# Sample-state updates as four 32-row matmuls on four row groups, with keys and values laid out through DRAM

## The chip, the core and the metric

The kernel runs on one core of a Trainium2 chip. A core has five engines that work at the same time and wait for each other by semaphores: PE (TensorE, matmuls; PEld is its weight load), DVE (VectorE), ACT (ScalarE), POOL (GpSimd) and SP (SyncE, which here only issues DMA transfers). SBUF is the on-chip memory of 128 partitions; PSUM holds matmul results in eight banks of 128 partitions by 512 fp32 numbers. TensorE is an array of 128 rows (over which a matmul sums) by 128 columns; a matmul may use a part of the rows (a row group of 32 or 64) or of the columns (a column group). The metric is device time in microseconds, the median of three runs.

## The reference

One layer of a hybrid decoder is computed for a prompt (512 tokens) and for a sample batch (8 sequences of 4 new tokens): an input projection, an mLSTM branch with 4 heads of dimension 512, a sliding-window attention branch, a gated merge and a layer norm. The change touches the sample's mLSTM only. For each of 8 sequences and 4 heads there is a matrix memory C of 512 by 512 that is read and updated:

```python
num = einsum('bhts,bhsd->bhtd', s, v) + inter[..., None] * einsum('bhtk,bhkv->bhtv', q, C)
...
C_new = decay[..., None, None] * C + einsum('bhsk,bhsv->bhkv', w[..., None] * k, v)
```

So every C tile (1 MB) is loaded, multiplied with 4 queries, updated by a product of 4 weighted keys with 4 values, and stored. The output C is returned for all 32 pairs of sequence and head. All numbers are fp32; to keep that precision in TensorE's faster fp32r format, operands are split into a high and a low part and the needed products of parts are summed.

## The kernel before

The large projections take most of the time. `paired` (L695) goes through a list of pairs of output column blocks; for each pair it runs seven half products (`half_product`, L654: sixteen matmuls at L662 and eight at L664, 272 columns each) that use three PSUM banks, with sums of weight blocks (`prepare`, L642), splits of weights (`split`, L198 on ACT and L199 on DVE) and a gathering of the results (`gather`, L672 to L691) around them. Splits are prepared up to three half products ahead (L704).

After each half product, `tick()` (L127) lets each generator in `live` run up to its next `yield`. That is how smaller work is mixed into the projections. `samples()` (L1208) is one such generator: it takes the heads one after another and runs `sample_head` (L1155). A planner that simulates the engines then sets the final order of each engine's instructions from dependences and priorities; `tc.high_priority` moves instructions ahead in it, and `tc.issue_after` puts an instruction behind a named one on its engine. Each engine, and each DMA queue, then works strictly in that order. All transfers of this part are issued by SP.

`sample_prep` (L1060) loads queries, keys and values of a head (L1065), and makes two tiles of 128 rows by 512: `kA` (L1092 and L1093) holds the weighted keys of all 32 tokens four times, as high, high, low and low parts; `V4` (L1102 and L1105) holds the values as high, low, high and low parts. A product over the 128 rows is so a sum over 32 tokens and over all four pairs of parts.

`sample_head` then loops over the 8 sequences b. A C tile is loaded one sequence ahead (L1057). POOL makes `qz` (L1172, L1173), the queries of b among zeros, and `Ab` (L1175), which is `kA` with the rows of all other sequences set to zero by a mask. Four matmuls (L1188) on the four column groups of the array multiply the queries with the four 128-row parts of C and add into the PSUM bank `pC`, which is held for the whole head; they come up in the profile as eight records. Then, for each of the four parts of C, one matmul of 128 rows, 128 columns and 512 moving columns (L1194) makes the update, though only 16 of its 128 rows are not zero, and one DVE instruction (L1195) scales the C tile by the decay and adds it. Two parts are done in one tick and two in the next. The stores (L1165) are issued by SP in the next sequence's turn. `sample_finish` (L1133) works on `pC` at the end of a head.

PSUM banks come from two pools of four: `sm()` (L104), which the sample's work uses, `pC` and the update's results among it, and `bank()` (L214), which the half products use.

Of the kernel before, what the change touches and what calls it, by code (L numbers as in the profile page):

```python
# [15 lines left out]
F32 = mybir.dt.float32  # L16
F32R = mybir.dt.float32r
# [22 lines left out]
SLOPES = [float(np.float32(2.0 ** (-8.0 * (h + 1) / AH))) for h in range(AH)]  # L40


C_ID, C_TRI, C_M8, C_SM, C_SEL, C_DIST, C_SB, C_Q, C_N = 0, 128, 256, 264, 296, 328, 584, 716, 844


def constants():
    c = np.zeros((128, C_N), np.float32)
    p = np.arange(128)
    c[:, C_ID:C_ID + 128] = np.eye(128)
    c[:, C_TRI:C_TRI + 128] = np.where(p[None, :] >= p[:, None], 0.0, NEG)  # L50
    dist = p[:, None] + 128 - np.arange(256)[None, :]
    c[:, C_DIST:C_DIST + 256] = np.where((dist >= 0) & (dist < 128), dist, 1.0e32)
    t = p % 4
    sd = 128 + t[:, None] - np.arange(132)[None, :]
    slope = np.array(SLOPES, np.float32)[p // 4]
    sb = -(slope[:, None] * sd.astype(np.float32)).astype(np.float32)
    c[:, C_SB:C_SB + 132] = np.where((sd >= 0) & (sd < 128), sb, NEG)
    tok = p % 32
    c[:, C_M8:C_M8 + 8] = (tok[:, None] // 4 == np.arange(8)[None, :])
    tt = np.arange(32)  # L60
    same = (tok[:, None] // 4 == tt[None, :] // 4) & (tok[:, None] <= tt[None, :])
    c[:, C_SM:C_SM + 32] = np.where(same, 0.0, NEG)
    c[:, C_SEL:C_SEL + 32] = (tok[:, None] == tt[None, :])
    c[:, C_Q:C_Q + 128] = np.where(tok[:, None] == tok[None, :], 0.25, 0.0)
    return c

# [7 lines left out]
def _build(tc, nc, i, o, es):  # L74
# [25 lines left out]
    def nm(s):  # L100
        count[0] += 1
        return f"{s}_{count[0]}"

    def sm():  # L104
        return psB.tile([128, 512], F32, tag="sm", name=nm("sm"))
# [4 lines left out]
    def r32(ap):  # L110
        return ap.bitcast(F32)
# [62 lines left out]
    d_t = dr.tile([16, 128, T], F32, name="d_t")  # L174
    d_y = dr.tile([16, 128, T], F32, name="d_y")
    d_o = dr.tile([12, 128, T], F32, name="d_o")

    def kview(name):
        return i[name].rearrange("(kt p) c -> p kt c", p=128)
# [860 lines left out]
    sp = {}  # L1040

    def open_samples():
        for name, bufs in (("s1p", 1), ("sC", 2), ("sw", 2)):
            sp[name] = pool(esS, name, bufs)

    def st1(shape, tag, dt=F32, p="s1p"):
        return sp[p].tile(shape, dt, tag=tag, name=nm(tag))
# [2 lines left out]
        return r32(st1([128, 512], "rep", F32R)[:])  # L1050

    def w512():
        return sp["sw"].tile([128, 512], F32, tag="w", name=nm("w"))

    def load_C(h, b):
        ct = sp["sC"].tile([128, 4, 512], F32, tag="C", name=nm("C"))
# [3 lines left out]
    def sample_prep(h, r):  # L1060
        qs = st1([128, 4, NS], "qs", p="sw")
        ks_, vs = (st1([128, 4, NS], t_) for t_ in ("ks", "vs"))
        hc = slice(h * 4, h * 4 + 4)
        for t_, d_ in ((qs, d_q), (ks_, d_k), (vs, d_v)):
            nc.sync.dma_start(t_[:], d_[hc, :, SEQ:T].rearrange("c p t -> p c t"))  # L1065
        nh_ = w512()
        nh = nh_[:8]
        nc.sync.dma_start(nh, i["state_mlstm_n"][:, h, :])
        yield
        yield  # L1070
        rep = rep_tile()
        G.tensor_copy(rep.rearrange("p (c r t) -> p c r t", c=4, r=4), ks_[:].unsqueeze(2).to_broadcast([128, 4, 4, NS]))
        yield

        pS, pb = sm(), sm()
        for c in range(4):
            PE.matmul(pS[:, 0:NS], rep[:, c * 128:c * 128 + 128], qs[:, c], start=(c == 0), stop=(c == 3))
        PE.matmul(pb[:, 0:NS], row_h[:, h:h + 1].to_broadcast([68, 128]), nM[:, SEQ:T], start=True, stop=True)
        pk = sm()
        for c in range(4):  # L1080
            PE.transpose(pk[:, c * 128:c * 128 + 128], rep[:, c * 128:c * 128 + 128], ident)
        ds = st1([128, NS], "ds")
        V.tensor_tensor(out=ds[:], in0=pb[:, 0:NS], in1=cc[:, C_SM:C_SM + NS], op=ALU.add)
        A.activation(ds[:], ds[:], AF.Exp, bias=colT1[:, 4, 0, h:h + 1])
        V.tensor_tensor(out=ds[:], in0=pS[:, 0:NS], in1=ds[:], op=ALU.mult)
        Pst = st1([128, NS], "Pst", F32R)
        A.copy(Pst[:], ds[:])
        V.tensor_tensor(out=Pst[64:128], in0=ds[64:128], in1=r32(Pst[64:128]), op=ALU.subtract)

        wcol = colT2[:, 4, 2, h:h + 1]  # L1090
        kA = st1([128, 512], "kA", F32R)
        A.activation(kA[:], pk[:], AF.Copy, scale=wcol)  # L1092
        V.scalar_tensor_tensor(kA[64:128], pk[64:128], wcol[64:128], r32(kA[64:128]), op0=ALU.mult, op1=ALU.subtract)  # L1093
        repv = rep_tile()
        G.tensor_copy(repv.rearrange("p (c r t) -> p c r t", c=4, r=4), vs[:].unsqueeze(2).to_broadcast([128, 4, 4, NS]))
        yield

        pvv = sm()
        for c in range(4):
            PE.transpose(pvv[:, c * 128:c * 128 + 128], repv[:, c * 128:c * 128 + 128], ident)  # L1100
        V4 = st1([128, 512], "V4", F32R)
        A.copy(V4[:], pvv[:])  # L1102
        for q in (1, 3):
            rr = slice(q * 32, q * 32 + 32)
            V.tensor_tensor(out=V4[rr], in0=pvv[rr], in1=r32(V4[rr]), op=ALU.subtract)  # L1105

        pn = sm()
        for c in range(4):
            PE.transpose(pn[:, c * 8:c * 8 + 8], nh[:, c * 128:c * 128 + 128], ident[:8, :8])
        nT = st1([128, 4, NB], "nT")  # L1110
        V.tensor_copy(nT[:].rearrange("p c b -> p (c b)"), pn[:, 0:32])
        yield
        pq = sm()
        for c in range(4):
            PE.matmul(pq[:NS, 0:NB], qs[:, c], nT[:, c], start=(c == 0), stop=(c == 3))
        pd = sm()
        PE.matmul(pd[:NS, 0:2], Pst[:], ones_r[:], start=True, stop=True)
        pnn = sm()
        PE.matmul(pnn[:8, :], m8r[:], kA[:], start=True, stop=True)
        den = st1([32, 16], "den", p="sw")  # L1120
        V.scalar_tensor_tensor(den[:, 0:8], pq[:NS, 0:NB], colT2[0:32, 4, 1, h:h + 1], cc[0:32, C_M8:C_M8 + 8],
                               op0=ALU.mult, op1=ALU.mult, accum_out=den[:, 8:9])
        V.tensor_tensor(out=den[:, 9:10], in0=pd[:NS, 0:1], in1=den[:, 8:9], op=ALU.add)
        V.scalar_tensor_tensor(nh, nh, dcc[:, h:h + 1], pnn[:8, :], op0=ALU.mult, op1=ALU.add)
        nc.sync.dma_start(n_s[:, h, :], nh)
        yield
        pN = sm()
        PE.matmul(pN[:NS, :], Pst[:], V4[:], start=True, stop=True)
        num = st1([32, 512], "num")[:]
        A.copy(num, pN[:NS, :])  # L1130
        r.update(kA=kA, V4=V4, den=den, num=num, qs=qs)

    def sample_finish(h, r, pC):  # L1133
        qh, ql = (st1([128, 512], t_, F32R) for t_ in ("rep", "qcl"))
        col = colT2[:, 4, 1, h:h + 1]
        A.activation(qh[:], pC[:], AF.Copy, scale=col)
        V.scalar_tensor_tensor(ql[:], pC[:], col, r32(qh[:]), op0=ALU.mult, op1=ALU.subtract)
        gs = st1([128, 4, NS], "gs", p="sw")
        nc.sync.dma_start(gs[:], d_g[h * 4:h * 4 + 4, :, SEQ:T].rearrange("c p t -> p c t"))
        yield  # L1140
        num, den = r["num"], r["den"]
# [13 lines left out]
    def sample_head(h):  # L1155
# [12 lines left out]
        for b in range(NB):  # L1168
            ct = nxt

            qz = st1([128, 4, NS], "qz", p="sw")
            G.memset(qz[:], 0.0)  # L1172
            G.tensor_copy(qz[:, :, b * 4:b * 4 + 4], r["qs"][:, :, b * 4:b * 4 + 4])  # L1173
            Ab = st1([128, 512], "rep", F32R)
            G.tensor_scalar(Ab[:], r32(r["kA"][:]), cc[:, C_M8 + b:C_M8 + b + 1], None, op0=ALU.mult)  # L1175
            for j in range(4 + b % 2):
                yield
                if j == 0:
                    store()
                elif j == 2 and b + 1 < NB:  # L1180
                    with tc.issue_after(state["load"].ins):
                        nxt = load_C(h, b + 1)
            if b == 0:
                pC = sm()

            with tc.high_priority(offset=3000):
                for c in range(4):
                    PE.matmul(pC[c * 32:c * 32 + 32, :], qz[:, c], ct[:, c],  # L1188
                              start=(b == 0), stop=(b == NB - 1), tile_position=(0, c * 32))
            for c in range(4):  # L1190
                if c == 2:
                    yield
                pu = sm()
                PE.matmul(pu[:], Ab[:, c * 128:c * 128 + 128], r["V4"][:], start=True, stop=True)  # L1194
                V.scalar_tensor_tensor(ct[:, c], ct[:, c], dcb[:, h, b:b + 1], pu[:], op0=ALU.mult, op1=ALU.add)  # L1195
                if c % 2:
                    stores.append((C_s[b, h, (c - 1) * 128:c * 128 + 128, :].rearrange("(c p) v -> p c v", p=128),
                                   ct[:, c - 1:c + 1]))
        yield
        store()  # L1200
        while h not in gated:
# [669 lines left out]
```

## Time and profile before

| what | value |
|---|---|
| median of three runs | 2505.25 us (2504.25 to 2505.31) |
| span of the profiled execution, first to last instruction | 2501.3 us |
| mean granted TensorE clock | 0.997 |
| PE busy, weight loads busy | 2467.7 us, 2410.1 us |
| DVE, ACT, POOL busy | 1817.9, 1242.3, 388.8 us |
| memory traffic | 457.36 MB, mean 183 GB/s |
| first to last update matmul (L1194) | 1077.2 to 1757.4 us |
| update matmuls, C scale-and-add on DVE | 128 each |

The profile is of one execution; its span does not hold what lies before the first and after the last instruction, so it is 3.95 us below the median; no other time of that execution is given. Busy times of different engines overlap. Rows name the line, engine, operation and tiles (`out<-in`); a tile stands under the name it was made with, so the update's PSUM tile is `sm`, its keys (`Ab`) are `rep` and its values (`V4`) are `V`. A shape such as `128*32` before the element counts of a matmul is the rows and columns of the array that it uses. `A <- B` in a list of waits says that A waited for B.

### The profile page before, as it was taken

The numbers are of one execution on the slowest core, as the hardware profiler recorded it, in microseconds if no ns is written. First come the engines' busy times: TensorE is split into PE (matmuls) and PEld (weight loads), VectorE is DVE, ScalarE is ACT, GpSimd is POOL, SyncE is SP. The second block draws the span as 40 slices with busy tenths as digits, with TensorE's granted clock in tenths as the row PEclk, the third lists the DMA queues.
The fourth block names the chain that finished last, engine by engine and source line by source line (L and its number), as shares of the span: only waits on it lengthen the run. The fifth ranks groups of instructions, "written<-read, shape, count | busy, mean of one in ns | idle before, by whom it ended". The sixth has DMA issues, their size and how long they took to land.

```text
span 2501.3 us, 48664 instructions
## 1 busy us (share of the span) xinstructions
PE 2467.7 (99%) x19542; PEld 2410.1 (96%) x19542; DVE 1817.9 (73%) x2785; ACT 1242.3 (50%) x2033; POOL 388.8 (16%) x376
## 2 busy tenths in 40 slices
PE   8999999999999999999999999999999999999997
PEld 8899999999999999999999999999999999999997
DVE  7867677677677687787877888787855654766667
ACT  6457677666667665443433444444633333334431
POOL 2111221121121111121111122211000000110101
PEclk9999999999999999999999999999999999999998
DMA  6677666666666655477677567577745546788776
GB/s 166 153 185 187 149 152 159 156 146 164 153 148 161 149 126 150 113 208 226 184 216 222 168 198 216 172 221 216 247 157 177 193 146 213 210 228 257 211 217 195
DMA packets 551796, 457.36 MB, mean 183 GB/s; under 512 B 45073, under 2 KB 451777, under 8 KB 551313
## 3 DMA queue, kind: packets, MB, share of 16 engines
q1 hardware_dynamic: 534672, 394.73, 53.2%
q0 software_dynamic: 15696, 57.15, 11.8%
q8 instruction: 153, 2.51, 0.4%
q10 hardware_dynamic: 1200, 2.36, 0.3%
q14 instruction: 75, 0.61, 0.1%
HBM read 313.82 MB, written 94.22 MB: 163 GB/s over the span
## 4 chain that ended last, share of the span: by engine, by line
PE 49%; issue 4%; DMA 2%; DVE 2%; ACT 0%; SPq 0%; POOL 0%; DVEq 0%; POOLq 0%; ACTq 0%
PE bank L662 22%; PE bank L664 11%; PE bank L207 6%; PE sm L1375 2%; PE sm L1194 1%; PE sm L1188 1%; PE sm L1407 1%; PE sm L1420 1%; PE sm L207 1%; PE sm L1737 1%; DMA tx<-d_y 1%; DMA ty<-d_y 0%; DMA d_y<-c 0%; DMA tx<-d_brm 0%; DVE wl L199 0%
## 5 line engine op out<-in xcount | busy, mean ns | idle before, releaser
L198 ACT CAST wh<-raw 128x1024 fp32r<-128x1024 f32 x632 | 661.6, 1048 | 820.6 <-PE bank L662 680.1
L199 DVE TENSOR_TENSOR wl<-raw,wh 128x1024 fp32r<-128x1024 f32 x632 | 779.7, 1234 | 238.5 <-ACT wh L198 205.6
L662 PE MATMUL bank<-xk,wh 128*128 128x272 f32 x2336 | 322.6, 288 | 1.4 <-DVE ev L687 1.4
L642 DVE TENSOR_TENSOR raw<-raw,raw 128x1024 f32<-128x1024 f32 x238 | 302.9, 1275 | 8.2 <-DMA raw<-in_w_in 2.2
L662 PEld LDWEIGHTS bank<-xk,wh 128*128 128x128 f32 x2336 | 304.0, 188 | 3.5 <-DVE ev L687 1.6
L681 POOL TENSOR_TENSOR ev<-p,ev 128x272 f32<-128x272 f32 x82 | 123.6, 1507 | 582.5 <-ACT ev L680 537.0
L664 PE MATMUL bank<-xk,wl 128*128 128x272 f32 x1168 | 171.8, 287 | 0.8 <-DVE wl L199 0.8
L662 PE MATMUL bank<-s1h,wh 128*128 128x272 f32 x656 | 170.0, 291 | 0.9 <-ACT wh L198 0.8
L662 PE MATMUL bank<-s4h,wh 128*128 128x272 f32 x656 | 169.4, 290 | 0.5 <-ACT wh L198 0.2
L662 PE MATMUL bank<-n3l,wh 128*128 128x272 f32 x656 | 169.0, 289 | 0.0
L662 PE MATMUL bank<-n3h,wh 128*128 128x272 f32 x656 | 169.0, 289 | 0.0
L662 PE MATMUL bank<-n2h,wh 128*128 128x272 f32 x656 | 168.9, 289 | 0.0
L662 PE MATMUL bank<-n2l,wh 128*128 128x272 f32 x656 | 168.6, 289 | 0.0
L662 PE MATMUL bank<-s1l,wh 128*128 128x272 f32 x656 | 168.5, 289 | 0.0
L662 PE MATMUL bank<-s4l,wh 128*128 128x272 f32 x656 | 168.3, 288 | 0.0
L664 PEld LDWEIGHTS bank<-xk,wl 128*128 128x128 f32 x1168 | 155.8, 188 | 1.1 <-DVE wl L199 1.0
L662 PE MATMUL bank<-a11h,wh 128*128 128x272 f32 x584 | 150.2, 289 | 1.2 <-ACT wh L198 1.2
L662 PE MATMUL bank<-a11l,wh 128*128 128x272 f32 x584 | 149.9, 288 | 0.0
L207 PE MATMUL bank<-bh,wl 128*128 128x272 f32 x704 | 147.5, 289 | 1.2 <-DVE wl L199 1.2
L207 PE MATMUL bank<-bl,wh 128*128 128x272 f32 x704 | 148.6, 289 | 0.0
L207 PE MATMUL bank<-bh,wh 128*128 128x272 f32 x704 | 148.0, 289 | 0.0
L640 POOL DMA_DIRECT2D raw<-raw x90 | 77.6, 863 | 313.4 <-DVE sums L783 142.4
(488 smaller groups left out, 5623.2 us busy)
## 6 DMA issues: line engine op xcount, KB each, us to landing
raw<-in_w_in SPq DMA_DIRECT2D x296, 512.0 KB, 4.5
raw<-raw POOLq DMA_DIRECT2D x90, 512.0 KB, 5.0
C<-in_state_mlstm_C SPq DMA_DIRECT2D x32, 1024.0 KB, 6.6
out<-C SPq DMA_DIRECT2D x64, 512.0 KB, 3.1
raw<-in_w_proj_a SPq DMA_DIRECT2D x32, 512.0 KB, 5.1
raw<-in_w_proj_m SPq DMA_DIRECT2D x32, 512.0 KB, 5.9
raw<-in_w_out SPq DMA_DIRECT2D x32, 512.0 KB, 4.4
d_v<-ev SPq DMA_DIRECT2D x16, 272.0 KB, 4.7
```

The source lines that it names most:

```text
L198: A.copy(wh[:, k:k + n], raw[:, k:k + n])
L199: V.tensor_tensor(out=wl[:, k:k + n], in0=raw[:, k:k + n], in1=r32(wh[:, k:k + n]), op=ALU.subtract)
L207: PE.matmul(ps[f][:, :w], a[:, kk], b(k, c, w), start=(k == 0 and n == 0), stop=(k == 15 and n == 2))
L640: G.dma_start(out=w[out][:], in_=w[b][:], accum_op=ALU.add)
L642: V.tensor_tensor(out=w[out][:], in0=w[a][:], in1=w[b][:], op=ALU.add)
L662: PE.matmul(ps, wh[:, k], x(p, k), start=(first and k == 0 and p == 0), stop=False, skip_group_check=True)
L664: state["end"] = PE.matmul(ps, wl[:, k], x(0, k), start=False, stop=(k == 7), skip_group_check=True)
L681: G.tensor_tensor(out=c22, in0=p1, in1=c11, op=ALU.subtract)
L1188: PE.matmul(pC[c * 32:c * 32 + 32, :], qz[:, c], ct[:, c], start=(b == 0), stop=(b == NB - 1), tile_position=(0, c * 32))
L1194: PE.matmul(pu[:], Ab[:, c * 128:c * 128 + 128], r["V4"][:], start=True, stop=True)
L1375: PE.matmul(pp[:, 0:258], a[:, b * 128:b * 128 + 128], b_[:, b, f], start=(b == 0 and n == 0), stop=(b == 3 and n == 2))
L1407: PE.matmul(pp[:, 0:n], x_[c][:, b * 128:b * 128 + 128], y_[c][:, b * 128:SEQ], start=(c == 0 and m == 0), stop=(c == 3 and m == 2))
```

## The change

The zeros are taken out of the update. Two neighbouring sequences (8 tokens, 4 parts each) fill 32 rows. After `kA` and `V4` are made, eight DMAs (`rows_to`) write them to a DRAM buffer `d_kv` in the order of such pairs. For each pair g of sequences two DMAs (`load_kv`) bring them back: `KB`, 128 by 128, holds on row group c the 32 rows of keys for part c of C; `VB`, 128 by 512, holds the 32 rows of values four times, once on each row group. The first pair is loaded at the end of `sample_prep`, each later one in the turn of the sequence before it.

POOL's mask now works on `KB` (128 columns in place of 512) and keeps the one of the two sequences that is meant; its result has two buffers. The four updates of a C tile become four matmuls of 32 rows, 128 columns and 512 moving columns on the four row groups, each into its own `sm` bank, all four issued together behind the query matmuls at their priority. The four DVE instructions follow in one tick, and the `yield` that stood between them comes after them. `pC` is taken from `bank()` in place of `sm()`. Some tiles move to pools with one buffer, `V4` shares the buffer of `ql`, and the constants become two columns wider for the new mask.

```diff
+    c[:, C_M2:C_M2 + 2] = (p[:, None] % 8 // 4 == np.arange(2)[None, :])
...
+    d_kv = dr.tile([MH, 2, 4, 32, 512], F32, name="d_kv")
...
-        for name, bufs in (("s1p", 1), ("sC", 2), ("sw", 2)):
+        for name, bufs in (("s1p", 1), ("sC", 2), ("sw", 2), ("sv", 2)):
...
     def w512():
-        return sp["sw"].tile([128, 512], F32, tag="w", name=nm("w"))
+        return st1([128, 512], "w")
+
+    def rows_to(h, n, t_):
+
+        for q in range(4):
+            nc.sync.dma_start(d_kv[h, n, :, q * 8:q * 8 + 8, :],
+                              r32(t_[q * 32:q * 32 + 32]))
+
+    def load_kv(h, g):
+
+        kb, vb = st1([128, 128], "KB", F32R, "sv"), st1([128, 512], "VB", F32R, "sv")
+        nc.sync.dma_start(r32(kb[:]), d_kv[h, 0, g].rearrange("p (c x) -> c p x", c=4))
+        nc.sync.dma_start(r32(vb[:]), d_kv[h, 1, g].unsqueeze(0).to_broadcast([4, 32, 512]))
+        return kb, vb
...
-        V4 = st1([128, 512], "V4", F32R)
+        V4 = st1([128, 512], "qcl", F32R)
...
+        with tc.issue_after(state["load"].ins):
+            rows_to(h, 0, kA)
+            rows_to(h, 1, V4)
...
-        r.update(kA=kA, V4=V4, den=den, num=num, qs=qs)
+        r.update(kv=load_kv(h, 0), den=den, num=num, qs=qs)
...
+            if b % 2 == 0:
+                kb, vb = r["kv"]
+            Ab = st1([128, 128], "Ab", F32R, "sw")
+            masked = G.tensor_scalar(Ab[:], r32(kb[:]), cc[:, C_M2 + b % 2:C_M2 + b % 2 + 1], None, op0=ALU.mult)
             qz = st1([128, 4, NS], "qz", p="sw")
-            G.memset(qz[:], 0.0)
+            with tc.issue_after(masked.ins):
+                G.memset(qz[:], 0.0)
             G.tensor_copy(qz[:, :, b * 4:b * 4 + 4], r["qs"][:, :, b * 4:b * 4 + 4])
-            Ab = st1([128, 512], "rep", F32R)
-            G.tensor_scalar(Ab[:], r32(r["kA"][:]), cc[:, C_M8 + b:C_M8 + b + 1], None, op0=ALU.mult)
...
                         nxt = load_C(h, b + 1)
+                        if b % 2:
+                            r["kv"] = load_kv(h, b // 2 + 1)
             if b == 0:
-                pC = sm()
+                pC = bank()
...
+                pus = [sm() for _ in range(4)]
+                for c in range(4):
+                    own = slice(c * 32, c * 32 + 32)
+                    PE.matmul(pus[c][:], Ab[own], vb[own], start=True, stop=True, tile_position=(c * 32, 0))
             for c in range(4):
-                if c == 2:
-                    yield
-                pu = sm()
-                PE.matmul(pu[:], Ab[:, c * 128:c * 128 + 128], r["V4"][:], start=True, stop=True)
-                V.scalar_tensor_tensor(ct[:, c], ct[:, c], dcb[:, h, b:b + 1], pu[:], op0=ALU.mult, op1=ALU.add)
+                V.scalar_tensor_tensor(ct[:, c], ct[:, c], dcb[:, h, b:b + 1], pus[c][:], op0=ALU.mult, op1=ALU.add)
...
+            yield
```

More of the change, by code (lines that the diff above doesn't have):

```diff
@@ L40 @@
 SLOPES = [float(np.float32(2.0 ** (-8.0 * (h + 1) / AH))) for h in range(AH)]
-C_ID, C_TRI, C_M8, C_SM, C_SEL, C_DIST, C_SB, C_Q, C_N = 0, 128, 256, 264, 296, 328, 584, 716, 844
+C_ID, C_TRI, C_M8, C_SM, C_SEL, C_M2, C_DIST, C_SB, C_Q, C_N = 0, 128, 256, 264, 296, 328, 330, 586, 718, 846
 def constants():
@@ L1137, in sample_finish @@
         V.scalar_tensor_tensor(ql[:], pC[:], col, r32(qh[:]), op0=ALU.mult, op1=ALU.subtract)
-        gs = st1([128, 4, NS], "gs", p="sw")
+        gs = st1([128, 4, NS], "gs")
         nc.sync.dma_start(gs[:], d_g[h * 4:h * 4 + 4, :, SEQ:T].rearrange("c p t -> p c t"))
```

## Prediction

> **What bounds the kernel now.** I read the page's busy line first, then the stretch in which the changed lines run (the update matmuls start between 1077 and 1757 us), its chain, and last the single instructions.
>
> ```profile
> PE 2467.7 (99%) x19542; PEld 2410.1 (96%) x19542; DVE 1817.9 (73%) x2785; ACT 1242.3 (50%) x2033; POOL 388.8 (16%) x376
> ```
>
> ```profile
> 1060.00:1780.00 720.00, 719.13 (x5585) 677.87 (x5585) 571.09 (x681) 298.22 (x373) 138.95 (x144) 1.00 0.67 202
> ```
>
> The columns of the second row are the stretch, its length, the busy time of PE, PEld, DVE, ACT and POOL, the granted clock, the DMA share and GB/s. PE is busy 719.13 of 720 us at full clock; DVE has 149 us free, POOL 581 us, the DMA engines a third. So in this stretch the kernel's time is PE's, and PE time taken out there shortens the end one for one, unless another wait takes its place. The chain through the stretch agrees:
>
> ```profile
> by line: PE bank L662 58.2%; PE bank L664 28.9%; PE sm L1194 5.0%; PE sm L1188 4.4%; PE sm L1077 0.4%; PE sm L1081 0.3%; ACT wh L198 0.3%; issue 0.3%; PE sm L1144 0.3%; PE sm L1115 0.2%; PE sm L1151 0.2%; PE sm L1100 0.2%; ACT L1237 0.2%; A
> ```
>
> L1194, the update, is 5.0% of 720 us = 36 us of the chain; all else named there is left alone. 36 us is the most that the change could win. After 1780 us PE stays the bound (1780 to 1880 us below), so what is won is kept:
>
> ```profile
> 1780.00:1880.00 100.00, 99.28 (x793) 98.45 (x792) 70.09 (x143) 50.32 (x93) 3.90 (x7) 1.00 0.65 220
> ```
>
> **The update's price on PE today.** The rows of the groups in the stretch (instructions | busy, mean ns | idle before them), and one update in order of time (start, length):
>
> ```profile
> L1194 PE MATMUL sm<-V,rep 128*128 128x512 f32 x128 | 48.1, 421 | 0.0
> L1188 PE MATMUL sm<-C,qz 128*32 128x512 f32 x256 | 34.1, 605 | 0.0
> L1195 DVE SCALAR_TENSOR_TENSOR C<-C,dcb,sm 128x512 f32<-128x512 f32 x128 | 90.1, 741 | 2.9 <-PE sm L1194 1.8
> L1175 POOL TENSOR_SCALAR rep<-kA,cc 128x512 fp32r<-128x512 f32 x32 | 57.9, 1810 | 108.3 <-PE sm L1194 72.3 <-DVE C L1195 15.2 <-DVE wl L199 10.1
> ```
>
> ```profile
> 1256.74 0.41 PE L664 MATMUL bank<-n2h,wl 128*128 128x272 f32 x2
> 1257.08 1.07 PE L1188 MATMUL sm<-C,qz 128*32 128x512 f32 x8
> 1258.08 0.73 PE L1194 MATMUL sm<-V,rep 128*128 128x512 f32 x2
> 1258.65 2.16 PE L662 MATMUL bank<-xk,wh 128*128 128x272 f32 x16
> 1260.65 1.17 PE L664 MATMUL bank<-xk,wl 128*128 128x272 f32 x8
> 1261.65 0.39 PE L1194 MATMUL sm<-V,rep 128*128 128x512 f32 x1
> 1261.88 0.28 PE L662 MATMUL bank<-n3h,wh 128*128 128x272 f32 x1
> ```
>
> Matmuls are pipelined, so I count from start to start. The sixteen L662 take 2.00 us, 0.125 each. A lone update takes 1261.65 to 1261.88 = 0.23; the two behind L1188 take 1258.08 to 1258.65 = 0.57, that is 0.11 over 2 x 0.23: the first waits for its weights, which elsewhere load behind the matmul before. Four updates are 0.57 + 2 x 0.23 = 1.03 us, and 128/4 = 32 groups make 33.0 us. The two L664 ahead of L1188 take 0.34 where two slots are 0.25: leaving one shape of the array for another costs 0.09 of draining. A switch is thus 0.09 + 0.11 = 0.20 us. L1188 already shows matmuls side by side: eight of 605 ns, on four column groups, take 1.00 us together (1257.08 to 1258.08).
>
> The trace holds 32-row matmuls too, one row group at a time, between full ones:
>
> ```profile
> 987.67 0.59 PE L982 MATMUL sm<-vb,PT 128*128 128x256 f32 x2
> 988.19 0.69 PE L983 MATMUL sm<-vas,PT 32*128 32x256 f32 x2
> 988.82 0.70 PE L982 MATMUL sm<-vb,PT 128*128 128x256 f32 x2
> 989.45 0.69 PE L983 MATMUL sm<-vas,PT 32*128 32x256 f32 x2
> ```
>
> A pair of L982 entered without a switch takes 987.67 to 988.19 = 0.52, entered by one 0.63: again 0.11. The 32-row pair takes 0.63, as the 128-row pair does: fewer rows make a matmul no shorter; only running several at once can win.
>
> **The change, part by part.** (1) *Update on PE.* Removed: 32 x 1.03 us. Added: four matmuls of 32 rows on four row groups, 512 columns each. If they run at once like L1188's column groups: 0.11 (weights, as now after L1188) + 0.23 (one matmul) + 0.03 (three staggers, an estimate: L1188's eight records of 605 ns all lie within 1.07 us, so within a round of four the starts are hundredths apart) + 0.09 + 0.11 (the switch back to 128 rows, which the old updates did not need, being of that shape) = 0.57 us. Saved 1.03 - 0.57 = 0.46, times 32 = 14.7 us. Ends: with the switch back hidden 0.37, saved 21 us; all four one after another 0.11 + 0.92 + 0.20 = 1.23, lost 6.4 us. I take 14.7, since both the concurrency of four (L1188) and the switch (L983, L1188) stand in rows; only row groups with full width have none.
>
> The Trainium skill ("TensorEngine Tiling (Array Packing)", Key Properties) says that changing the tiling mode drains the engine; the 0.09 us ahead of L1188 agrees. The Trainium skill's page "TensorE: Matmul & The Clock Gate" (Measured speedup vs the span model) gives 3.07 times for four row tiles with 512 columns: by that, as an estimate, 1.03/3.07 = 0.34 us and 22 us saved, which is nearly the end without a switch back; no run shown here has such a group yet.
>
> (2) *DVE.* The four L1195 stay (128 x 0.741 us) but come as one burst of 2.96 us instead of two of 1.48. Behind a burst waits the splitting of weights and the gathering of half products; a half product is 2.00 + 1.00 = 3.0 us on PE and operands are prepared up to three ahead, so 1.5 us more fits: 0, and if that cover were gone, 32 x 1.5 = 48 us.
>
> (3) *POOL.* The masked keys shrink from 512 to 128 columns: 1.81 us each (L1175) to an estimate of a quarter, 0.45: 44 us less on an engine with 581 free: 0. It now waits for a transfer; behind it on POOL stand the clearing of the next query tile and L681 of the half products, with one to three half products of room.
>
> (4) *PSUM.* The sample's accumulating bank moves from the four `sm` banks to the four `bank` banks for a whole head; the update now takes all four `sm` at once, which nothing else in the stretch wants except the same generator 15 us earlier or later. Three `bank` banks stay for the pairs, each using three. A bank is next needed two half products (6 us) after its last product, and its reader takes 0.44 us, 3.4 us behind a full burst: 0. If not covered, see the rivals.
>
> (5) *SP queue and DMA.* Per head 8 stores of 64 KB and 4 x 2 loads (64 and 256 KB): 64 issues in all and 0.5 + 1.28 = 1.8 MB per head, 7.1 MB, or 35 us at 202 GB/s; at that rate's share of 0.67 they add 0.03. An issue costs SP as one of a C tile does, 0.38 us (its instructions, then SP's longest waits: total, times, longest):
>
> ```profile
> L1057 SPq DMA_DIRECT2D C<-in_state_mlstm_C x31: 367/380/848, 1071.1 to 1726.4; - x31
> ```
>
> ```profile
> SPq L1165 <- DVE C L1195: 131.0, 52, 8.3
> SPq L185 <- DVE raw L642: 101.1, 30, 6.9
> SPq L1057 <- DMA out<-C: 53.4, 22, 4.9
> ```
>
> 64 x 0.38 = 24 us of a queue that spends hundreds waiting: 0. The pair loads of one head (issued an iteration of 15 to 20 us ahead) need at most 4.9 (wait of the C load before them) + 3 x 0.38 + 8.0 (longest landing below) = 14 us: covered. The first pair of a head is not so far ahead (the first head's values and update, then two landing times of small transfers, the second that of the sample's loads from DRAM, L1065):
>
> ```profile
> L1105 DVE TENSOR_TENSOR V<-sm,V x2: 684/690/696, 1067.2 to 1067.9; 32x512 fp32r<-32x512 f32 x2
> L1194 PE MATMUL sm<-V,rep x2: 397/448/499, 1077.2 to 1077.6; 128*128 128x512 f32 x2
> ```
>
> ```profile
> d_brm<-gs SPq DMA_DIRECT2D x4, 64.0 KB, 1.8
> DMA to landing us min/median/max: 2.0/5.1/8.0
> ```
>
> In the first head the values are ready at 1068.6 and the update starts at 1077.2, 8.6 us later. The new way needs 8 x 0.38 = 3.0 of issue, 1.8 of landing, 0.8 of issue, 5.1 (2.0 to 8.0) of landing and 0.4 of mask: 11.1 us (8.0 to 14.0). So the update comes 2.5 us late (0 to 5.4) if PE's order stays; the order is made by a planner that knows of transfers and can put product matmuls ahead. Four heads: 0 to 22 us; I take 2 us, near the lower end, because PE waited 0.0 for L1188 and L1194, whose C tiles are transfers planned in just this way.
>
> (6) Constants two columns wider, tiles moved between pools, single buffers for tiles used once per head: 0; their users stand a head (170 us) apart.
>
> Sum: -14.7 + 2 = -12.7 us. The profiled execution's span is 2501.3 us; the median of the runs is 2505.25, 3.95 above it, which I carry: 2488.6 + 3.95 = 2492.5 us.
>
> **Rivals.** (A, forecast) as summed, 2492.5. (B) The switch back is hidden, as the concurrent groups drain one by one: 21.1 - 2 = 19 us, 2486; against it, every change of shape shown cost 0.11 and 0.09. The 3.07 times of the Trainium skill's page on TensorE falls into this case. (C) The four weight loads come in turn, 0.11 each, since all four want the full 128 columns, where L1188's want 32: 3 x 0.11 - 0.03 more, 0.87 us a group, 5 us saved, less 2: 2502. (D) The change does not do what it says: row groups do not run at once, 1.23 us a group: 2505.25 + 6.4 + 2 = 2513.7. For it: no row shows full-width row groups together. (E, slower, one mechanism) SP stands still at each head: the loads of a pair's keys must wait for the stores to land and the stores for the values, and the weight loads behind them on SP come late. It decides from 14.7/4 = 3.7 us per head; at the bound of 5.4 for the keys plus 3.0 + 1.8 for the weights behind them, 4 x 10.2 - 14.7 = 26 us: 2531. Against it: PE found its weights ready after the 131 us that SP stood at L1165. (F) Three `bank` banks are too few: 720/21 = 34 pairs, and 0.43 us per pair eats the gain; a half product's wait each time would be 34 x 3.0 - 12.7, 2595. Against it the 6 us in (4).
>
> **How the numbers follow.** A 0.55, B 0.18, C 0.06, D 0.07, E 0.10, F 0.04. What a measurement tells from no change is 0.2%, 5.0 us: 2500.2 to 2510.3. Faster: A and B: 0.73. Within: C and the mild part of E, 0.03: 0.09. Slower: D, F and 0.07 of E: 0.18. Range: from 2482 (B with no wait at the heads) to 2510 (E at some 5 us per head); it leaves out D, F and 0.07 of E, 0.18.
>
> **What would show it.** Four matmuls 32*128 starting within hundredths of each other, and L662 some 0.45 us after the first with one slow weight load (A); without it (B); starts 0.1 apart (C); 0.23 apart (D). PE's idle time ahead of the update by a POOL or DMA releaser at the first update of a head, or ahead of L662 by ACT or DMA (E); L662 waiting for DVE `ev` (F). The stretch from the first to the last update should shrink by some 13 us, with DVE's L1195 in bursts of 2.96. I am wrong if the group takes over 1 us, or if PE's busy share there falls below 0.99.

## The result, and the profile after

The changed kernel takes 2495.1 us (median of four runs, 2491.2 to 2497.6) against 2505.3 before: a ratio of 0.9958, 95% interval 0.9944 to 0.9972, so 10.2 us or 0.4% faster. The forecast was 2492.5. Two later measurements of it, each beside the kernel before on one chip, gave 0.9948 (0.9934 to 0.9963) and 0.9960 (0.9947 to 0.9972).

Line numbers are higher by up to 24 in the new kernel: L662 and L664 are now L664 and L666, L1188 is L1211, the update L1194 is L1216, its DVE part L1195 is L1218, and the mask L1175 is L1192. In the columns as shown of before, the stretch from 1060 to 1780 us:

```profile
1060.00:1780.00 720.00, 713.23 (x5661) 669.82 (x5660) 579.95 (x690) 304.38 (x381) 124.62 (x148) 1.00 0.72 217
```

In the same 720 us there are now 5661 matmul records in place of 5585, so more of the half products are done by 1780 us; but PE has 6.8 us of idle time where it had 0.9, and the DMA share went from 0.67 to 0.72. What the stretch gained is seen between two points of work that both kernels have: the first matmul of the first head's preparation (L1077, now L1092) and the first matmul of the projection behind the stretch (L207, now L209). 5710 matmul records lie between them in both. First and last start stand behind the three durations; the first two rows are of before, the others of after:

```profile
L1077 PE MATMUL sm<-qs,rep x8: 276/276/296, 1058.9 to 1059.7; 128*128 128x32 f32 x8
L207 PE MATMUL bank<-bh,wh x78: 283/288/376, 1794.7 to 1849.5; 128*128 128x272 f32 x78
L1092 PE MATMUL sm<-qs,rep x8: 276/276/297, 1058.5 to 1059.3; 128*128 128x32 f32 x8
L209 PE MATMUL bank<-bh,wh x90: 284/287/373, 1784.8 to 1849.7; 128*128 128x272 f32 x90
```

1058.9 to 1794.7 is 735.8 us before, 1058.5 to 1784.8 is 726.3 us after: 9.5 us less. The groups of the update on PE, on DVE and on POOL (the last by minimum, median and maximum):

```profile
L1216 PE MATMUL sm<-VB,Ab 32*128 32x512 f32 x128 | 16.4, 499 | 5.4 <-DMA VB<-d_kv 5.4
L1218 DVE SCALAR_TENSOR_TENSOR C<-C,dcb,sm 128x512 f32<-128x512 f32 x128 | 87.8, 741 | 5.2 <-PE sm L1216 4.1
L1192 POOL TENSOR_SCALAR Ab<-KB,cc x32: 600/721/3201, 1069.6 to 1708.5; 128x128 fp32r<-128x128 f32 x32
```

PE's busy time for the 128 updates fell from 48.1 to 16.4 us; DVE's 128 instructions take 741 ns each as before. One update in order of time:

```profile
1101.31 0.92 PE L666 MATMUL bank<-n3h,wl 128*128 128x272 f32 x6
1102.16 1.07 PE L1211 MATMUL bank<-C,qz 128*32 128x512 f32 x8
1103.15 0.50 PE L1216 MATMUL sm<-VB,Ab 32*128 32x512 f32 x4
1103.59 0.39 PE L664 MATMUL bank<-s4h,wh 128*128 128x272 f32 x1
1103.82 0.29 PE L664 MATMUL bank<-s4l,wh 128*128 128x272 f32 x1
1103.94 0.29 PE L664 MATMUL bank<-s4h,wh 128*128 128x272 f32 x1
```

Four matmuls of 490 ns each lie within 0.50 us: they run at once. From the first one's start to the next half product 0.43 us pass (1103.15 to 1103.59 in the rounded rows), and from that one's first matmul to its second it is 0.23 in place of 0.125. That is the 0.11 of waiting for weights that the prediction reads behind every change of shape, here 0.10. The group so costs 0.43 + 0.10 = 0.53 us where four updates took 1.03; 0.43 and 0.23 are also the medians of all 32 groups.

Against this stands a new wait, at the first update of the first head:

```profile
1075.82 1.06 PE L1211 MATMUL bank<-C,qz 128*32 128x512 f32 x8
1081.94 0.89 PE L1216 MATMUL sm<-VB,Ab 32*128 32x512 f32 x4 [5.05 <-DMA VB<-d_kv]
```

```profile
PE sm L1216 <- DMA VB<-d_kv: 5.4, 2, 5.1
POOL Ab L1192 <- DMA KB<-d_kv: 168.9, 15, 15.2
```

PE stands 5.1 us for the values of the first pair, and 0.4 us at the second head. POOL's waits for keys, 169 us, are long, but no PE wait for POOL's keys (`Ab`) stands in the list: they are those of an engine that is done early. SP's transfers show the way that the values took, and the windows around the wait show the clock (the last three columns are the granted clock, the DMA share and GB/s):

```profile
1067.60 2.52 SPq L1060 DMA_DIRECT2D d_kv<-qcl  x4
1073.91 0.54 SPq L1067 DMA_DIRECT2D VB<-d_kv  x1
1074.55 0.42 SPq L635 DMA_DIRECT2D raw<-in_w_in  x1
1075.02 0.58 SPq L1072 DMA_DIRECT2D C<-in_state_mlstm_C  x1
```

```profile
1076.40:1081.90 5.50, 0.49 (x8) 0.00 (x0) 2.24 (x2) 0.00 (x0) 0.00 (x0) 1.00 1.03 206
1081.90:1085.30 3.40, 3.36 (x15) 2.95 (x16) 2.56 (x4) 0.00 (x0) 0.00 (x0) 0.50 0.60 211
```

The stores are issued from 1067.6 to 1070.1, SP waits for their landing and issues the load of VB at 1073.9, and the update can start at 1081.9, eight microseconds later, with all DMA engines busy (share 1.03) while a weight block and a C tile are on their way beside it. Then PE runs at half clock for 3.4 us, which costs another 1.7 (half of that time). The Trainium skill ("TensorE: Matmul & The Clock Gate", What's actually happening) says that an idle window of some 3.4 us brings the clock down to one half; the 0.50 here agrees. In other runs shorter waits, of 2.4 to 2.6 us, did it too, as the last section has it.

One more difference lies far behind, at 2150 us. It is in the profile before too, with 0.5 us:

```profile
DVE raw L644 <- DMA raw<-in_w_proj_m: 4.1, 1, 4.1
PE bank L209 <- DVE wl L201: 4.0, 1, 4.0
```

```profile
2150.00:2156.00 6.00, 3.93 (x17) 3.93 (x18) 5.71 (x9) 1.37 (x2) 0.94 (x1) 0.52 0.71 123
```

A weight block landed late, PE stood for 4.0 us and went on at half clock (0.52 over these 6 us). The profiled execution was the slowest of the four (2497.55 us, its span 2495.7), and this may be a part of it; whether the change causes it is a question for the experiments.

### The profile page after: what moved, and what is told of

Read it like the earlier page. It is cut to its first block, busy times and chain, and to the rows that moved or that the text cites. A ratio compares the mean times of both kernels' runs of the same rounds, so it can differ in the third digit from the quotient of the medians.

```text
span 2495.7 us, 48772 instructions
## 1 busy us (share of the span) xinstructions
PE 2453.8 (98%) x19542; PEld 2394.0 (96%) x19542; DVE 1817.8 (73%) x2785; ACT 1244.1 (50%) x2033; POOL 373.1 (15%) x376
## 3 DMA queue, kind: packets, MB, share of 16 engines
q8 instruction: 154, 2.52, 0.4%
## 5 line engine op out<-in xcount | busy, mean ns | idle before, releaser
L664 PE MATMUL bank<-xk,wh 128*128 128x272 f32 x2336 | 325.0, 290 | 0.9 <-DVE ev L689 0.9
L664 PEld LDWEIGHTS bank<-xk,wh 128*128 128x128 f32 x2336 | 304.3, 189 | 4.2 <-issue 2.6
L666 PE MATMUL bank<-xk,wl 128*128 128x272 f32 x1168 | 172.4, 288 | 0.8 <-DVE wl L201 0.8
L664 PE MATMUL bank<-s1h,wh 128*128 128x272 f32 x656 | 169.1, 291 | 0.2 <-ACT wh L200 0.2
L664 PE MATMUL bank<-n3h,wh 128*128 128x272 f32 x656 | 169.1, 289 | 0.0
L664 PE MATMUL bank<-n2h,wh 128*128 128x272 f32 x656 | 168.2, 289 | 0.6 <-ACT wh L200 0.6
L664 PE MATMUL bank<-s4h,wh 128*128 128x272 f32 x656 | 168.3, 290 | 0.1
L664 PE MATMUL bank<-n3l,wh 128*128 128x272 f32 x656 | 167.9, 287 | 0.0
L664 PE MATMUL bank<-n2l,wh 128*128 128x272 f32 x656 | 167.5, 287 | 0.0
L664 PE MATMUL bank<-s1l,wh 128*128 128x272 f32 x656 | 167.2, 287 | 0.0
L664 PE MATMUL bank<-s4l,wh 128*128 128x272 f32 x656 | 167.0, 287 | 0.0
L666 PEld LDWEIGHTS bank<-xk,wl 128*128 128x128 f32 x1168 | 156.6, 188 | 1.1 <-DVE wl L201 1.0
L664 PE MATMUL bank<-a11h,wh 128*128 128x272 f32 x584 | 150.8, 290 | 2.6 <-ACT wh L200 2.5
L209 PE MATMUL bank<-bh,wl 128*128 128x272 f32 x704 | 148.5, 291 | 4.7 <-DVE wl L201 4.7
L664 PE MATMUL bank<-a11l,wh 128*128 128x272 f32 x584 | 149.6, 289 | 0.0
L209 PE MATMUL bank<-bh,wh 128*128 128x272 f32 x704 | 148.8, 290 | 0.0
L209 PE MATMUL bank<-bl,wh 128*128 128x272 f32 x704 | 148.6, 290 | 0.0
L664 PEld LDWEIGHTS bank<-n3h,wh 128*128 128x128 f32 x656 | 123.3, 188 | 1.9 <-issue 1.4
```

Source lines behind the costliest of these rows:

```text
L209: PE.matmul(ps[f][:, :w], a[:, kk], b(k, c, w), start=(k == 0 and n == 0), stop=(k == 15 and n == 2))
L664: PE.matmul(ps, wh[:, k], x(p, k), start=(first and k == 0 and p == 0), stop=False, skip_group_check=True)
L666: state["end"] = PE.matmul(ps, wl[:, k], x(0, k), start=False, stop=(k == 7), skip_group_check=True)
```

## The experiments

The kernel before ran beside every variant on the same chip, 2505.2 to 2505.8 us in the median, and ratios are against it. The changed kernel itself ran on the chip of the order alone, the one row group and the first update later at the first head (2493.4 us), and on that of the second form of two sets and of the last kernel with the first update later (2494.6); the other variants ran on a third chip and are set against 2493.4. The theory at this point: the four row groups give 16 us, the first head's late values take some 7 back, and the stall at 2150 us is chance.

**The changed kernel again** (no edit).

> The changed kernel once more, unchanged, for a second profile. Theory 1: the two stalls of the first profile are of different kinds. The wait of the first update for its values (5.1 us, at 1077 us) is built into the order of SP and PE and comes again, within 1 to 2 us; the stall at 2150 us (4 us of waiting for a w_proj_m block and some 1.5 us at half clock) is the chance of one execution's transfers and is gone or small, so the span is some 4 us shorter than the first one's 2495.7. Theory 2: the stall at 2150 us is caused by the change, since all that follows comes 10 us earlier and meets the same transfers; it comes again with 4 to 6 us. By both 2491 to 2498 us.

Measured: 2493.4 us (2490.2 to 2498.0). PE waited 5.2 us for VB at the first update again. The half clock behind it lasted longer than in the first profile:

```profile
1083.70:1089.90 6.20, 6.19 (x27) 5.76 (x28) 3.86 (x5) 1.05 (x1) 0.93 (x3) 0.50 0.79 284
```

That is 6.2 us, worth some 3 us. In a third profile of the changed kernel (below) it was 4.5 us behind a wait of 4.9. So the first head's late values cost 6.8, some 8 and some 7 us in the three profiles. At 2150 us PE waited 2.5 us, and the span was 2496.2: the stall did not go, and the span did not shrink as theory 1 had it. PE's wait there was 0.5 us before, 4.0, 2.5 and 2.6 in the three profiles of the changed kernel, 5.1 and 0.7 in two profiles of one and the same variant (the first update of every head later), 2.5 in the kernel before with the new order alone, 2.3 in the second form of two sets, 4.9 with the values ahead of the keys, and 0.8 or less in others. It differs as much within one kernel as between kernels, and it comes without the row groups and the way through DRAM. So the change is not needed for it. Whether it makes it more frequent, single profiles can't tell; but the medians fell by 10.2 to 12.4 us, not less than the 9.5, 7.9 and 9.6 us by which the stretch of the updates shrank in the three profiles.

**The order alone.**

```diff
             if b == 0:
-                pC = sm()
+                pC = bank()
...
+                pus = [sm() for _ in range(4)]
+                for c in range(4):
+                    PE.matmul(pus[c][:], Ab[:, c * 128:c * 128 + 128], r["V4"][:], start=True, stop=True)
             for c in range(4):
-                if c == 2:
-                    yield
-                pu = sm()
-                PE.matmul(pu[:], Ab[:, c * 128:c * 128 + 128], r["V4"][:], start=True, stop=True)
...
+            yield
```

> The kernel before with only the order of the change: pC in a bank of the half products' pool, the four 128-row updates together behind the queries, the four DVE instructions in one tick; no layout through DRAM and no row groups. If terms 2 and 4 of the prediction are right (costs 0), this is the time before within 2 us: 2503 to 2507, the update group 0.34 + 3 x 0.23 = 1.03 us. Rival: three banks or the burst on DVE cost something that the row groups' gain hid; then it is slower than before, by 0.4 us or more per pair of columns, 14 us and up.

Measured: 2506.0 us, ratio 0.9999 (0.9989 to 1.0008). An update in its profile:

```profile
1096.57 1.07 PE L1188 MATMUL bank<-C,qz 128*32 128x512 f32 x8
1097.56 1.20 PE L1192 MATMUL sm<-V,rep 128*128 128x512 f32 x4
1098.60 0.29 PE L662 MATMUL bank<-s4h,wh 128*128 128x272 f32 x1
```

The four take 1097.56 to 1098.60 = 1.04 us, as before. Three banks for the half products, four `sm` banks at once and the burst on DVE cost nothing that can be measured (the interval is -2.8 to +2.0 us; the stretch from the first L1077 to the first L207 takes 735.4 us where it took 735.8).

**One row group for all four.**

```diff
...
-        nc.sync.dma_start(r32(kb[:]), d_kv[h, 0, g].rearrange("p (c x) -> c p x", c=4))
-        nc.sync.dma_start(r32(vb[:]), d_kv[h, 1, g].unsqueeze(0).to_broadcast([4, 32, 512]))
+        nc.sync.dma_start(r32(kb[:]), d_kv[h, 0, g])
+        nc.sync.dma_start(r32(vb[:]), d_kv[h, 1, g])
...
-                    PE.matmul(pus[c][:], Ab[own], vb[own], start=True, stop=True, tile_position=(c * 32, 0))
+                    PE.matmul(pus[c][:], Ab[:, c * 128:c * 128 + 128], vb[:], start=True, stop=True, tile_position=(0, 0))
```

> The changed kernel with all four matmuls of 32 rows on the same row group: keys as 32 by 512, values as 32 by 512 without the fourfold copy, so a quarter of the value bytes, and the mask over 512 columns. If the gain is the four row groups running at once, the group takes 0.11 + 4 x 0.23 until the last one's end and 0.20 for the way back, 1.23 us in place of 0.54: 22 us slower than the changed kernel, 2515 to 2519, slower than the kernel before too. Rival: the gain comes from fewer rows or from the new order and place; then within 5 us of the changed kernel.

Measured: 2506.3 us, ratio 1.0002 (0.9993 to 1.0012).

```profile
1096.65 1.06 PE L1211 MATMUL bank<-C,qz 128*32 128x512 f32 x8
1097.64 1.20 PE L1216 MATMUL sm<-VB,rep 32*128 32x512 f32 x4
1098.77 0.39 PE L664 MATMUL bank<-s4h,wh 128*128 128x272 f32 x1
1099.00 0.29 PE L664 MATMUL bank<-s4l,wh 128*128 128x272 f32 x1
```

The group takes 1.13 us to the next half product and 0.10 more there: 1.23, to the hundredth what was expected. So the gain is the concurrency of row groups; matmuls of 32 rows on one group are no cheaper than of 128. The total was missed: the whole kernel is 12.9 us slower than the changed one, not 22. The groups alone make (1.23 - 0.53) x 32 = 22 us; 7 to 9 of these come back because no update waits for VB (VB is a quarter as large, and PE's list of waits has no VB) and no half clock follows. That leaves 13 to 15. The stretch from L1092 to L209 bears it out: it takes 740.5 us, 14.2 and 12.6 more than in the first two profiles of the changed kernel. Against the kernel before, the groups would make it 6 us slower; its stretch is 4.7 us longer (740.5 against 735.8), but the whole runs show -1.8 to +3.0. Where the 3 us and more between them went I can't say.

**The set of four twice.**

```diff
-                for c in range(4):
+                for c in (0, 1, 2, 3, 0, 1, 2, 3):
```

> The changed kernel with each group of four row-group matmuls issued twice into the same banks; the second set writes the same numbers again, so it only doubles this one cost. If four matmuls cost one streaming of 512 columns and the rest of the 0.54 us is the change of shape, a group grows by 0.22 us, to 0.76, and the kernel by 7 us, to 2501. If the row groups shared something and a set of four took 0.4 us of its own, a group grows by 0.4 and the kernel by 13 us, to 2507.

Measured: 2501.5 us, ratio 0.9984 (0.9975 to 0.9993), 8.1 us over the changed kernel's 2493.4.

```profile
1103.50 1.07 PE L1211 MATMUL bank<-C,qz 128*32 128x512 f32 x8
1104.50 0.74 PE L1216 MATMUL sm<-VB,Ab 32*128 32x512 f32 x8
1105.16 0.39 PE L664 MATMUL bank<-s4h,wh 128*128 128x272 f32 x1
```

1104.50 to 1105.16 is 0.66 us where one set takes 0.43: four more matmuls cost 0.23 us, one streaming. By the prices that the prediction read off the kernel before, the other 0.30 of the 0.53 us are the first set's weights (0.11) and the way back to 128 rows: 0.09 of draining and 0.10 for weights. The last 0.10 is measured in the new rows; how the rest divides is not.

**Two sets of two.** First with a priority block for each set:

```diff
+            for c in range(4):
+                if c == 2:
+                    yield
+                if c % 2 == 0:
+                    with tc.high_priority(offset=3000):
+                        for c_ in (c, c + 1):
...
+                            PE.matmul(pus[c_][:], Ab[own], vb[own], start=True, stop=True, tile_position=(c_ * 32, 0))
```

> The changed kernel with the update in two sets of two row groups, a tick between them, as the kernel before had it. If a change of shape costs 0.20 us out and back and a set costs one streaming whatever its size, the second set costs 0.09 + 0.11 + 0.22 + 0.20 = 0.62 us, 32 times 0.62 = 20 us more than the changed kernel, 2513, which is more than the kernel before. Rival: the changes of shape hide behind the half products, and a set of two costs its streaming only: 7 us more, 2501.

Measured: 2592.2 us, 3.5% slower than before, far from both. The profile shows why:

```profile
1106.20 1.04 PE L1211 MATMUL bank<-C,qz 128*32 128x512 f32 x2
1107.17 0.49 PE L1222 MATMUL sm<-VB,Ab 32*128 32x512 f32 x1
1107.59 1.04 PE L1211 MATMUL bank<-C,qz 128*32 128x512 f32 x2
1108.57 0.50 PE L1222 MATMUL sm<-VB,Ab 32*128 32x512 f32 x1
1108.99 1.05 PE L1211 MATMUL bank<-C,qz 128*32 128x512 f32 x4
1109.98 0.40 PE L664 MATMUL bank<-s4h,wh 128*128 128x272 f32 x1
```

Queries and first set now stand in two blocks that count their priority back by the same 3000, and the planner mixed their instructions: one query matmul (two records), an update, one query matmul, an update, two query matmuls. Each piece of the queries takes 0.97 to 0.99 us, as all four together do, and each lone update 0.42. Queries and first set last 3.78 us in place of 1.4. So this run does not tell what a second set costs. The next one keeps the first set in the queries' block, behind them:

```diff
-                pus = [sm() for _ in range(4)]
-                for c in range(4):
+                pus = {}
+                for c in range(2):
...
+            for c in range(4):
+                if c == 2:
+                    yield
+                    with tc.high_priority(offset=3000):
+                        for c_ in (2, 3):
```

> Two sets of two row groups again, now with the first set right behind the four query matmuls, so that PE's order has them as queries, set, half product, set. If a change of shape costs 0.20 us out and back and a set costs one streaming whatever its size, the second set adds 0.09 + 0.11 + 0.22 + 0.20 = 0.62 us, 20 us in all: 2513. Rival: the second set's changes of shape hide behind the half products and it adds its streaming only: 2501.

Measured: 2515.1 us, ratio 1.0042 (1.0028 to 1.0056), 20.6 us over the changed kernel on the same chip (2494.6, below). A set of two takes 0.43 us to the next matmul like a set of four, so the second one adds all its changes of shape: 0.09 ahead of it, 0.43, and 0.10 behind, 0.62 us or 20 us for 32. Split in two ticks, as the kernel before had its updates, the same row groups make the kernel slower than before.

**The first update later.**

```diff
-            for j in range(4 + b % 2):
+            for j in range(4 + b % 2 + (2 if h == 0 and b == 0 else 0)):
```

> Two more ticks ahead of the first update of the first head, some 6 us of half products put before it; nothing else is changed. If the stall there is only the late values (theory 1), it goes: 5 us faster than the changed kernel, about 2490 us, PE's wait for VB under 0.5 us. Rival: the transfers behind each other on SP are the limit and the wait only moves to the weight blocks behind them; then no gain, 2495 us, and PE or DVE waits for a raw block near 1085 us.

Measured: 2490.1 us, ratio 0.9936 (0.9922 to 0.9951), 3.3 us faster than the changed kernel beside it and not 5. The wait at the first head is gone; but in this profile PE waited 2.7 us for VB at the third head, where the changed kernel had not. So I gave the two ticks to every head and took them back later in it:

```diff
-            for j in range(4 + b % 2):
+            for j in range(4 + b % 2 + {0: 2, 2: -1, 4: -1}.get(b, 0)):
```

> Two more ticks ahead of the first update of every head, given back by one tick less ahead of the third and the fifth, so that a head is as long as in the changed kernel. Theory 1: what is left of PE's waiting in the samples' stretch is the first pair's values, late at some head in every execution (head 1 by 5 us in two profiles, head 3 by 3 us in the profile of first_later). Then no update waits over 0.5 us and the time is that of first_later or up to 3 us less, 2487 to 2491. Rival: with the two shorter turns the later pairs' loads become late; then PE waits for VB or KB at the third or fifth update, 1 us and up each, and the time is 2492 and up.

Measured: 2488.5 us, ratio 0.9932 (0.9919 to 0.9945), although its profiled execution, the slowest of the six, had the longest of the stalls at 2150 us, 5.1. Once more, beside the changed kernel:

> The kernel of first_later_all again, beside the changed kernel on the same chip. If the 5 to 6 us of waiting at the heads' first updates is what it removes, it is 4 to 6 us faster than the changed kernel. Rival: the waits come back elsewhere in most executions; then within 2 us of it.

> The changed kernel, unchanged, for the comparison with the run before it and for a third profile. Theory: the first head's first update waits 5 to 6 us for VB once more; PE's wait near 2150 us differs from the 4.2 and 2.7 us of the other profiles.

Measured: 2486.6 us, ratio 0.9930 (0.9916 to 0.9943), against 2494.6, ratio 0.9960 (0.9947 to 0.9972): 8.0 us faster than the changed kernel and 19 us faster than the kernel before. In the profile of the changed kernel the first head waited again (5.0 us for VB) and the stall at 2150 us was 2.6. In that of the variant no update waits for a transfer. What its list has for the update is idle time of the weight load, 0.8 us each behind the queries, as the kernel before had it:

```profile
PEld sm L1216 <- issue: 26.8, 32, 0.8
POOL Ab L1192 <- DMA KB<-d_kv: 140.1, 13, 13.8
```

The stretch now shows the row groups without the wait:

```profile
L1092 PE MATMUL sm<-qs,rep x8: 190/276/276, 1058.7 to 1059.4; 128*128 128x32 f32 x8
L209 PE MATMUL bank<-bh,wh x104: 284/287/373, 1778.5 to 1849.7; 128*128 128x272 f32 x104
```

1058.7 to 1778.5 is 719.8 us where the kernel before took 735.8: 16.0 us less, which is what the groups were counted at.

8.0 us is more than the 4 to 6 expected: the expectation left out the half clock behind the wait, 4.5 us long in the profile beside it.

**The values ahead of the keys.** The blocks that make and store V4 and kA change places in `sample_prep`, and in `load_kv` VB is loaded first.

```diff
+        repv = rep_tile()
...
+        with tc.issue_after(state["load"].ins):
+            rows_to(h, 1, V4)
+        rep = rep_tile()
...
         with tc.issue_after(state["load"].ins):
             rows_to(h, 0, kA)
-            rows_to(h, 1, V4)
```

> The changed kernel with the values made and stored ahead of the keys, and the values' load issued ahead of the keys': the values' way through DRAM starts one tick, 3 us, earlier, and the keys' way as much later. If the first update waits for the values alone, the 5 us at head 1 shrink by 3 us, and the time is 2490 to 2492. If the way from the stores through SP to the update is what counts, whichever tile is last, the wait stays at 4 to 6 us, now for KB through POOL's mask, and the time is that of the changed kernel, 2493 to 2495.

Measured: 2502.6 us, ratio 0.9994 (0.9982 to 1.0006): slower than both expectations. Now the keys come last, and behind their load stands POOL's mask:

```profile
PE sm L1217 <- POOL Ab L1193: 7.5, 1, 7.5
POOL Ab L1193 <- DMA KB<-d_kv: 201.1, 13, 23.4
```

PE waits 7.5 us at the first head, and the profile has waits of 2 to 4 us ahead of the query matmuls of the second and third. It is the profile of the slowest of twelve executions, 2514.3 us, so these waits are longer than is usual; and with this edit the first head's product of queries and keys comes 10 us later (1068.8 in place of 1058.5) and its first update stands ahead of the query matmuls. The rival held in its main point, that a wait comes back whichever tile is last, but its time was 8 us too low, and why the whole is slower than the changed kernel is not shown.

## Why the prediction was right

The direction and the mechanism were right, and the time was inside the range, 2.6 us above the forecast. That it came so near is in part luck: the groups won 1.3 us more than forecast and the waits cost 5 more. By its steps:

(1) *Update on PE*: forecast 0.57 us a group and 14.7 us saved; measured 0.53, that is 33.0 - 32 x 0.53 = 16 us. The staggers are 0.01 in all, not 0.03. Rival B (the switch back hidden) is out: the next half product's first matmul takes its 0.10 more, and a second set behind the first adds 0.23 where the first costs 0.53. Rivals C and D are out by the same rows, and D's price, 1.23, is what one row group costs. The 3.07 times of the Trainium skill ("TensorE: Matmul & The Clock Gate", Measured speedup vs the span model) did not hold for the kernel: 1.03/0.53 is 1.9, because a group pays for its change of shape. The same section's figure of about 4 ns for each further tile agrees with four matmuls of 490 ns in 0.50 us.

(2) and (4) *DVE, PSUM*: 0, and 0 within 2.8 us measured with the order alone. Rival F is out.

(3) *POOL*: the mask takes 0.72 us in the median, not 0.45, and POOL waits 169 us for keys; it costs nothing, as said.

(5) *SP and DMA*: the term that was mis-sized. Forecast 2 us for all four heads; the waits were 5.1 and 0.4 us, and 1.7 of half clock behind the first. The way of the values was put at 11.1 us (8.0 to 14.0) and took 13.7, from the end of the values' last DVE instruction at 1068.2 to 1081.9: a store takes 0.59 us of SP (four in 2.52 with what lies between them), not 0.38, the landing of the stores was seen 3.8 us after the last one's issue and not 1.8, and VB could be used 8.0 us after its load was issued, the longest landing that the prediction showed, not the median 5.1. I had taken a value near the lower end because PE never waited for C tiles; but a C tile is loaded a whole turn ahead, and the first pair is not. That the clock falls after such a wait was in no term. The stretch of the updates shrank by 9.5 us, not by the 13 that were named as a sign, and PE's busy share from 1060 to 1780 us, 713.23 of 720, is 0.9906, just above the 0.99 under which the prediction would have called itself wrong. Rival E had the right place and the wrong cause: it was the values themselves that came late and not, in the main, the weight blocks behind them.

Sum: -16 + 5.1 + 0.4 + 1.7 = -8.8 us, where the medians show -10.2 with an interval of -7.0 to -14.0.

## What to carry to other kernels

Small matmuls on several row groups pay when they can be issued together: the set costs one streaming plus a change of shape in and out, so count the changes of shape first, and keep the order of the planner from mixing shapes. Operands that go out to DRAM and back need their whole way (issue, landing, wait in the queue, load at full DMA share) as lead, and the first one of a loop is the one without it; moving that one use of each head by two ticks added 8 us to the 11 of the change, on the same chip.

## What the runs showed that I had not expected

A column-group query matmul alone takes as long as four (0.97 us against 0.99, in the mixed order), and a lone 32-row matmul 0.42 as four do 0.43: leaving groups of the array unused saves no time. A wait of some 5 us costs 7 to 8, since the granted clock is 0.50 for the next 3.4 to 6.2 us. Shorter waits are not safe either: after waits of 2.4 to 2.6 us the clock went to 0.50 in four profiles (the order alone, the changed kernel's second and third, the values ahead of the keys); after three of 2.3 to 2.7 us it stayed at 1.00 (one with the first update later, two with the two sets of two). So here the length of the wait alone did not decide it. And one late weight block at 2150 us makes executions of one kernel differ: from L209's first matmul to PE's end, the two profiles of the kernel with every head's first update later took 695 and 689 us, 6 us apart, half of this change's effect, so that a single profile's span (2495.7 here) says less than the median.
